# Macaron encoder, fp32 on one core: other sources for the weight sums of the seven-product FFN, one pool for them, and the first block's second pair later

## The chip, the core and the metric

The kernel runs on one core of a Trainium2 chip. The metric is the device time of the whole kernel in microseconds (us). Five engines work side by side, each through its own queue of instructions: TensorE (PE in the profile; PEld are its weight loads), VectorE (DVE), ScalarE (ACT), GpSimd (POOL) and SyncE (SP). The last two do little here but issue DMAs: SP the plain loads of weights, POOL the accumulating DMAs, which add a source to a tile that is in the core's memory (SBUF) already.

## What is computed

A trunk of two layers over 528 tokens (512 and 16 learned ones) of width 1024. Each layer is an FFN, a mixer (gated linear attention beside softmax attention), and an FFN again; the change is in the weights of the four FFNs.

```python
def swiglu(x, w_gate, w_up, w_down):
    return (jax.nn.silu(x @ w_gate) * (x @ w_up)) @ w_down
...
    for l in range(DEPTH):
        h = h + 0.5 * swiglu(rmsnorm(h, norm_gains[l, 0]), ffn_w_gate[l, 0], ffn_w_up[l, 0], ffn_w_down[l, 0])
        h = h + mixer(rmsnorm(h, norm_gains[l, 1]), w_in[l], gla_w2[l], gla_b2[l], gla_gn[l],
                      q_norm[l], k_norm[l], w_pa[l], w_pb[l], b_merge[l], w_out[l], cos, sin)
        h = h + 0.5 * swiglu(rmsnorm(h, norm_gains[l, 2]), ffn_w_gate[l, 1], ffn_w_up[l, 1], ffn_w_down[l, 1])
```

The hidden width is 2816. Everything is float32, and outputs are float32.

## The kernel before

**Products.** A float32 product is made of three matmuls on rounded operands: each operand is split into a high part (rounded to fp32r) and a low part (the rest), and high·high, high·low and low·high are added up. For a weight tile of 128 x 1024 the high part (`whi`) is a cast on ScalarE (L342) and the low part (`wlo`) a subtraction on VectorE (L343).

**Seven products for eight.** The hidden chunks of 128 are taken in 11 pairs (`NPAIR`). For a pair, the gate and up weights are cut into 2 x 2 blocks 11, 12, 21, 22 (512 KB each), the activations into 2 x 2 as well (two halves of the rows, two halves of the tokens), and the block product is made with seven products (Winograd's form of Strassen's scheme) in the order "1627543" or close to it. Three of the seven take a block as it is: "1" takes 11, "2" takes 12, "4" takes 22 (`DIRECT`). Four take sums of blocks:

- "7": s3 = 21 − 11
- "6": s2 = s3 + 22, three blocks
- "5": s1 = 21 + 22, two blocks
- "3": s4 = s2 − 12

The down product of two pairs together (a group, `unit`) is cut the same way and has the same seven products; these are the "S" steps, with block numbers 11 to 14 (`NPAIR + g`), four groups in each FFN, 16 in all. Each step is 24 matmuls on TensorE. In a group, `ffn_steps` writes the order out by hand: the last pair's "7", the group's "1", the pair's "4" and "3", the rest of the group between, and the next pair's "1" and "2". Each S step multiplies a "form" of the two pairs' hidden chunks, which ScalarE and VectorE make after the pair's last product: a cast on ScalarE (L825) and the rest on VectorE (L826), then differences (L831 to L836).

**Where the sums come from** (`sums`, L291). When "1" of a pair or group comes up, ScalarE writes −11 into a tile of pool `wsa` (L284, `negative`); POOL accumulates 21 from DRAM onto it: s3. SP loads 22 into a tile of pool `wsb`, and POOL accumulates s3 onto it: s2. When "2" comes up (for a group: when "1" has been rounded), SP loads 21 into a tile of `wsb` and POOL accumulates 22 from DRAM: s1; and ScalarE writes −12 into `wsa` and POOL accumulates s2 onto it: s4. So a pair takes five loads (11, 12, 22 for "4", and 22 and 21 again), two negatives and four accumulates, and s2 comes after two accumulates in a chain. All accumulates are issued at L289, all loads at L279.

**Order and buffers.** `use` (L353) is called with each step: it makes the high and low parts of the weights a few steps ahead (`make`, up to four and one apart) and fetches two loads further (`fetch`). For the first pair after a group and for every group (`ahead`) the sums are begun as soon as "1" is fetched. The raw blocks have three slots (`raw`) and one apart (`xraw`) that every fourth raw block of the FFNs uses; negatives and loads for sums have three slots each. In the mixer, weights come as plain tiles (`wts`) through the same three raw slots. A load is issued once the slot's last reader, the `wlo` of an earlier block or a negative, is done.

**The first FFN's first block.** Pairs 0 and 1 come first as "F" steps. After the last of them, `hidden` (L781) makes the hidden chunks of both pairs one after the other: scaling by the norm's factor (VectorE, L785), silu (ScalarE, L508), product (VectorE, L802). Chunks of pair 0 go on as plain tiles (L513, L514), those of pair 1 as forms (L825 on).

Of the kernel before, what the change touches and what calls it, by code (L numbers as in the profile page):

```python
# [10 lines left out]
F32 = mybir.dt.float32  # L11
# [53 lines left out]
SQUARES = {(0, "2"): (0, 1, 2, 3), (1, "1"): (4, 5, 6, 7)}  # L65
EARLIEST = ((0, 0), 2, "1")

# [160 lines left out]
class Weights:  # L228
# [3 lines left out]
    def __init__(self, nc, after, raw, hi, lo, wts, win, wdn):  # L232
        self.nc, self.raw, self.hi_pool, self.lo_pool, self.wts, self.win, self.wdn = nc, raw, hi, lo, wts, win, wdn
        self.long = self.short = None
        self.loads = []
        for t, col in zip(PLAN, COLUMN):
            if t[0] == "op":
                self.loads.append(t[1:])
            elif col % SLAB == 0:
                self.loads.append(col // SLAB)  # L240
        self.at = {load: i for i, load in enumerate(self.loads)}
        self.made, self.fetched, self.got, self.summed, self.raws, self.second = 0, 0, {}, {}, {}, {}
        self.pos, self.behind, self.after = 0, None, after
        ops = [i for i, load in enumerate(self.loads) if not isinstance(load, int)]
        self.apart = set(ops[4::5])
        self.raw_apart = set([i for i in ops if self.loads[i][2] in DIRECT][3::4])
        self.extra = None
        firsts = lambda load: [NPAIR + g for g in range(SEVENS)] + [p + 1 for p in lasts(load[0] == (0, 0))]
        self.ahead = [i for i in ops if self.loads[i][2] == "1" and self.loads[i][1] in firsts(self.loads[i])]
        self.chained = {}  # L250

# [22 lines left out]
    def block(self, f, i, name, pool=None, tag="raw"):  # L274

        w = self.slab(tag, pool or self.raw, not pool and self.fetched in self.raw_apart, f"w{name}_{f[0]}{f[1]}_{i}", F32)
        first = f + (i, name) == (0, 0, 0, "11")
# [4 lines left out]
    def negative(self, f, i, name, w):  # L282
        t = self.long.tile([P, SLAB], F32, tag="wsa", name=f"{name}_{f[0]}{f[1]}_{i}")
        self.nc.scalar.activation(t, w, AF.Copy, scale=-1.0)  # L284
        return t

    def add(self, t, src):

        return self.nc.gpsimd.dma_start(t, src, accum_op=ALU.add).ins  # L289

    def sums(self, f, i, product, w):  # L291


        got, before = self.summed, None
        if product == "1":
            s3 = self.negative(f, i, "s3", w)
            self.add(s3, self.dram(f, i, "21"))
            s2 = self.block(f, i, "22", self.short, "wsb")
            before = self.add(s2, s3)
            got[f, i, "7"], got[f, i, "6"], self.second[f, i] = s3, s2, s2  # L300
            self.chained[f, i] = before
        if product == ("ready" if i >= NPAIR else "2"):
            before = self.chained.pop((f, i))
            s1 = self.block(f, i, "21", self.short, "wsb")
            with self.after(before if i >= NPAIR else None):
                self.add(s1, self.dram(f, i, "22"))
            got[f, i, "5"] = s1
        if product == "2":
            s4 = self.negative(f, i, "s4", w)
            self.add(s4, self.second.pop((f, i)))  # L310
            got[f, i, "3"] = s4

    def fetch(self, upto):

        while self.fetched < min(upto, len(self.loads)):
            load = self.loads[self.fetched]
            if isinstance(load, int):
# [3 lines left out]
            elif load[2] in DIRECT:  # L321
                w = self.raws[self.fetched] = self.block(*load[:2], DIRECT[load[2]])
                if load == EARLIEST:
                    self.sums(*load, w)
            self.fetched += 1

    def make(self, upto):
        nc = self.nc
        while self.made < min(upto, len(self.loads)):
# [16 lines left out]
            self.made += 1  # L346
            if not isinstance(load, int) and load != EARLIEST:
                if load[2] == "2" or load[2] == "1" and load[:2] not in self.chained:
                    self.sums(*load, w)
                elif load[2] == "1" and load[1] >= NPAIR:  # L350
                    self.sums(*load[:2], "ready", w)

    def use(self, j):  # L353
        while self.ahead and self.ahead[0] < self.fetched:
            i = self.ahead.pop(0)
            self.sums(*self.loads[i], self.raws[i])
        n = self.room(j)
# [30 lines left out]
def build(tc, ctx, xt, wts, win, wdn, par, w2, const, umask, out):  # L388
# [280 lines left out]
    def ffn(l, f, norm, done, following):  # L669
# [221 lines left out]
        for i, step in enumerate(steps):  # L891
# [8 lines left out]
            elif step[0] == "F":  # L900
# [3 lines left out]
                if step[1:] == (1, "1"):  # L904
                    for j in range(KC // 2):
                        norm.pair(j)
                elif step[1]:
                    rs = factor.pop()
                    for q in range(4):
                        hidden(made[q // 2], q // 2, q % 2)  # L910
            elif step[0] == "O":
# [374 lines left out]
    def block_pools():  # L1286
        pools = open_pools("left", wsa=3, wsb=3, xraw=1, xwhi=1, xwlo=1)
        W.long, W.short, W.extra = pools["wsa"], pools["wsb"], pools
        return pools
# [264 lines left out]
```

## Time and profile before

| | us |
|---|---|
| time, median of three runs (lowest, highest) | 2190.57 (2187.82, 2195.3) |
| the profiled execution: its time | 2200.36 |
| the profiled execution: its span | 2198.6 |
| TensorE busy | 2159.6 |
| VectorE busy | 1716.9 |
| ScalarE busy | 1326.6 |

The profile is of one execution. Its span runs from the first to the last instruction; its time has 1.8 us more around it. Instructions are grouped by line, engine, operation and tiles, without the tiles' numbers: `w<-win` is a load of a gate or up block, `w<-wdn` of a down block, `s<-w` a negative or an accumulate onto one, `w<-s` the accumulate of s3 onto a load, `raw<-wts` a mixer's weight. A bracket behind a row of a timeline holds the time that its engine was idle before it and what ended that time. The granted clock is the share of TensorE's full speed that it was given.

### The profile page before, as it was taken

What the parts mean: (1) busy time and instruction counts of PE and PEld (TensorE: products, weight loads), DVE (VectorE), ACT (ScalarE), POOL (GpSimd) and SP (SyncE); (2) the same over time, 40 slices, a digit from 0 to 9 for tenths busy, and PEclk for the clock granted to TensorE, in tenths of its full rate; (3) what the DMA queues carried; (4) which work ended last, traced back from release to release, by engine and by line L of the source; (5) the groups of instructions that cost most, each with busy time, mean ns of one, the idle gap of its engine ahead of it and who ended that gap; (6) DMA issues with size and microseconds to landing.
All of it is one profiled execution on the core that took longest, in us unless ns stands there. A gap on an engine that the chain in (4) does not pass through costs nothing.

```text
span 2198.6 us, 40509 instructions
## 1 busy us (share of the span) xinstructions
PE 2159.6 (98%) x16572; PEld 2075.3 (94%) x16572; DVE 1716.9 (78%) x2627; ACT 1326.6 (60%) x1964; POOL 203.5 (9%) x236
## 2 busy tenths in 40 slices
PE   9999999999999999999999999999999999999998
PEld 9999999989999999999999999999888889999997
DVE  7888876677977688888698888775789867888885
ACT  8665545455784575656575656454557937656554
POOL 1111100000000011111011111000000001111110
PEclk9999999999999999999999999999999999999999
DMA  9899953211115489999588999532221237999961
GB/s 275 197 232 223 227 134 122 81 59 58 42 48 162 116 211 222 233 237 222 160 198 214 221 234 227 144 125 77 68 68 48 79 113 199 222 221 241 226 170 64
DMA packets 99098, 353.01 MB, mean 161 GB/s; under 512 B 10976, under 2 KB 13280, under 8 KB 98912
## 3 DMA queue, kind: packets, MB, share of 16 engines
q0 software_dynamic: 33408, 121.65, 30.7%
q1 hardware_dynamic: 63424, 225.54, 30.3%
q10 hardware_dynamic: 2080, 3.23, 0.4%
q8 instruction: 130, 2.13, 0.4%
q14 instruction: 56, 0.46, 0.1%
HBM read 287.47 MB, written 2.10 MB: 132 GB/s over the span
## 4 chain that ended last, share of the span: by engine, by line
PE 70%; DVE 9%; ACT 8%; DMA 7%; issue 5%; POOL 0%; DVEq 0%; ACTq 0%; POOLq 0%
PE ss L745 20%; PE ss L864 15%; PE mm L525 13%; PE ss L525 11%; DMA w<-win 5%; DVE wlo L343 3%; PE sm L525 3%; PE ss L700 2%; ACT s L284 2%; ACT whi L342 2%; DMA w<-s 2%; PE sm L1233 1%; ACT t L508 1%; DVE c L760 1%; DMA s<-win 1%
## 5 line engine op out<-in xcount | busy, mean ns | idle before, releaser
L745 PE MATMUL ss<-xc,whi 128*128 128x264 f32 (+1 forms) x4608 | 841.0, 284 | 1.8 <-ACT whi L342 1.8
L745 PEld LDWEIGHTS ss<-xc,whi 128*128 128x128 f32 x4608 | 714.4, 189 | 2.8 <-ACT whi L342 2.0
L745 PE MATMUL ss<-xc,wlo 128*128 128x264 f32 (+1 forms) x2304 | 653.9, 284 | 0.0
L343 DVE TENSOR_TENSOR wlo<-w,whi 128x1024 fp32r<-128x1024 f32 (+1 forms) x299 | 364.0, 1218 | 110.5 <-ACT whi L342 109.6
L745 PEld LDWEIGHTS ss<-xc,wlo 128*128 128x128 f32 x2304 | 434.4, 189 | 0.1
L342 ACT CAST whi<-w 128x1024 fp32r<-128x1024 f32 (+1 forms) x299 | 312.9, 1046 | 200.2 <-PE ss L745 116.8
L525 PE MATMUL mm<-x,whi 128*128 128x264 f32 (+1 forms) x1712 | 383.3, 314 | 0.0
L864 PE MATMUL ss<-g,whi 128*128 128x264 f32 (+1 forms) x1792 | 339.4, 288 | 17.5 <-ACT g L825 12.4
L864 PEld LDWEIGHTS ss<-g,whi 128*128 128x128 f32 x1792 | 283.2, 192 | 23.5 <-ACT g L825 15.1
L525 PEld LDWEIGHTS mm<-x,whi 128*128 128x128 f32 x1712 | 278.2, 188 | 15.8 <-DVE x L514 0.2
L525 PE MATMUL mm<-x,wlo 128*128 128x264 f32 (+1 forms) x856 | 264.3, 313 | 0.0
L864 PE MATMUL ss<-g,wlo 128*128 128x264 f32 (+1 forms) x896 | 256.9, 287 | 0.0
L342 ACT CAST whi<-raw 128x1024 fp32r<-128x1024 f32 x126 | 132.0, 1047 | 142.9 <-PE mm L525 69.1
L343 DVE TENSOR_TENSOR wlo<-raw,whi 128x1024 fp32r<-128x1024 f32 x126 | 153.9, 1222 | 77.7 <-ACT whi L342 76.9
L342 ACT CAST whi<-s 128x1024 fp32r<-128x1024 f32 x116 | 122.0, 1051 | 138.4 <-PE ss L745 73.2
L864 PEld LDWEIGHTS ss<-g,wlo 128*128 128x128 f32 x896 | 171.8, 192 | 0.0
L343 DVE TENSOR_TENSOR wlo<-s,whi 128x1024 fp32r<-128x1024 f32 x116 | 141.6, 1221 | 35.4 <-ACT whi L342 35.4
L525 PEld LDWEIGHTS mm<-x,wlo 128*128 128x128 f32 x856 | 159.6, 188 | 7.5
L284 ACT ACTIVATE s<-w 128x1024 f32<-128x1024 f32 x116 | 122.8, 1059 | 70.9 <-DVE wlo L343 50.4
L868 DVE TENSOR_TENSOR h<-h,ss 128x528 f32<-128x528 f32 (+1 forms) x224 | 153.5, 695 | 6.4 <-PE ss L864 3.4
L525 PE MATMUL ss<-g,whi 128*128 128x264 f32 (+1 forms) x764 | 142.9, 302 | 1.3 <-ACT g L513 1.3
L525 PEld LDWEIGHTS ss<-g,whi 128*128 128x128 f32 x764 | 111.7, 188 | 6.9 <-ACT g L513 1.5
(300 smaller groups left out, 3337.4 us busy)
## 6 DMA issues: line engine op xcount, KB each, us to landing
w<-win SPq DMA_DIRECT2D x217, 512.0 KB, 5.7
raw<-wts SPq DMA_DIRECT2D x126, 512.0 KB, 3.4
w<-wdn SPq DMA_DIRECT2D x80, 512.0 KB, 5.5
w<-s POOLq DMA_DIRECT2D x58, 512.0 KB, 5.7
s<-w POOLq DMA_DIRECT2D x58, 512.0 KB, 8.0
s<-win POOLq DMA_DIRECT2D x42, 512.0 KB, 6.7
w<-win POOLq DMA_DIRECT2D x42, 512.0 KB, 8.1
s<-wdn POOLq DMA_DIRECT2D x16, 512.0 KB, 5.5
```

The costliest lines, as they stand in the source:

```text
L284: self.nc.scalar.activation(t, w, AF.Copy, scale=-1.0)
L342: nc.scalar.copy(hi[:, cs], w[:, cs])
L343: nc.vector.tensor_tensor(lo[:, cs], w[:, cs], hi[:, cs].bitcast(F32), ALU.subtract)
L508: prev_act[0] = S.activation(*args, **kw).ins
L525: TE.matmul(acc.half[i][:width], lhs, rhs[:, acc.spans[i]], start=first, stop=last)
L700: last = TE.matmul(acc[:, t, :w], a[:, j, k], v[b][:, r], start=k == 0 and r == 0 and i == 0, stop=k == len(x) - 1 and r == 1 and i == 2)
L745: TE.matmul(acc[:, j], a[:, j, k], b[:, at], start=bool(begin and k == 0 and i == 0), stop=k == len(x) - 1 and i == 2, skip_group_check=no ...
L760: V.tensor_tensor(st["c"][:, :, q], st["c"][:, :, q], acc, ALU.add)
L864: TE.matmul(acc[:, j], a[:, 2 * half + j, k], b, start=bool(begin and k == 0 and i == 0), stop=k == 1 and i == 2, skip_group_check=not begin)
L868: V.tensor_tensor(to, to, acc, ALU.add)
L1233: TE.transpose(tp[:, j * w + u * n : j * w + (u + 1) * n], pr[:n, (2 * c2 + j) * P : (2 * c2 + j + 1) * P], ident[:n, :n])
```

## The change

The sums come from other sources. s1 = 21 + 22 is made first: SP loads 21 (`base`) and POOL accumulates 22 (`base_sum`), for every group, for the third pair of the first FFN and for the first pair after a group begun two loads (`LEAD`) before "1" is fetched. When "1" is there, ScalarE writes −11 twice: onto the first, POOL accumulates 21 from DRAM (s3), onto the second s1, which gives s2 = 21 + 22 − 11 (`first_sums`). s4 is made as before (`last_sum`). A pair then takes four loads, three negatives and four accumulates, and s2 comes after one accumulate behind its negative. The pools `wsa`, `wsb` and `xraw` go; one pool `ws` of seven slots holds all sums, and all raw blocks go through the three slots of `raw`. In the first FFN the chunks of pair 1 are put off to the end of the next step and alternate with those of pair 0 in the code.

```diff
@@ -63,7 +63,7 @@
 STORES = (((0, 4), (4, 4)), ((0, 1), (1, 2), (3, 3), (6, 2)))
 RESERVED = [((l, f), 1, "5") for l, f in ((0, 1), (1, 0), (1, 1))]
 SQUARES = {(0, "2"): (0, 1, 2, 3), (1, "1"): (4, 5, 6, 7)}
-EARLIEST = ((0, 0), 2, "1")
+LEAD = 2
 
 
 def unit(begin, g):
@@ -231,7 +231,7 @@
 
     def __init__(self, nc, after, raw, hi, lo, wts, win, wdn):
         self.nc, self.raw, self.hi_pool, self.lo_pool, self.wts, self.win, self.wdn = nc, raw, hi, lo, wts, win, wdn
-        self.long = self.short = None
+        self.sum_pool = None
         self.loads = []
         for t, col in zip(PLAN, COLUMN):
             if t[0] == "op":
@@ -243,11 +243,17 @@
         self.pos, self.behind, self.after = 0, None, after
         ops = [i for i, load in enumerate(self.loads) if not isinstance(load, int)]
         self.apart = set(ops[4::5])
-        self.raw_apart = set([i for i in ops if self.loads[i][2] in DIRECT][3::4])
         self.extra = None
-        firsts = lambda load: [NPAIR + g for g in range(SEVENS)] + [p + 1 for p in lasts(load[0] == (0, 0))]
-        self.ahead = [i for i in ops if self.loads[i][2] == "1" and self.loads[i][1] in firsts(self.loads[i])]
-        self.chained = {}
+        self.bases, self.agenda = [], []
+        for i in ops:
+            f, p, product = self.loads[i]
+            if product == "1":
+                early = p >= NPAIR or f == (0, 0) and p == 2 or p - 1 in lasts(f == (0, 0))
+                at = i - LEAD * early
+                self.bases.append((at, (f, p)))
+                self.agenda += [(at, 0, (f, p))] + [(i, 1, (f, p))] * early
+        self.bases.sort()
+        self.agenda.sort()
 
     def dram(self, f, i, name):
         if i >= NPAIR:
@@ -273,55 +279,49 @@
 
     def block(self, f, i, name, pool=None, tag="raw"):
 
-        w = self.slab(tag, pool or self.raw, not pool and self.fetched in self.raw_apart, f"w{name}_{f[0]}{f[1]}_{i}", F32)
+        w = self.slab(tag, pool or self.raw, False, f"w{name}_{f[0]}{f[1]}_{i}", F32)
         first = f + (i, name) == (0, 0, 0, "11")
         for a in np.split(np.arange(SLAB), 2 if first else 1):
             self.nc.sync.dma_start(w[:, a[0] : a[-1] + 1], self.dram(f, i, name)[:, a[0] : a[-1] + 1])
         return w
 
     def negative(self, f, i, name, w):
-        t = self.long.tile([P, SLAB], F32, tag="wsa", name=f"{name}_{f[0]}{f[1]}_{i}")
+        t = self.sum_pool.tile([P, SLAB], F32, tag="ws", name=f"{name}_{f[0]}{f[1]}_{i}")
         self.nc.scalar.activation(t, w, AF.Copy, scale=-1.0)
         return t
 
     def add(self, t, src):
 
-        return self.nc.gpsimd.dma_start(t, src, accum_op=ALU.add).ins
-
-    def sums(self, f, i, product, w):
-
-
-        got, before = self.summed, None
-        if product == "1":
-            s3 = self.negative(f, i, "s3", w)
-            self.add(s3, self.dram(f, i, "21"))
-            s2 = self.block(f, i, "22", self.short, "wsb")
-            before = self.add(s2, s3)
-            got[f, i, "7"], got[f, i, "6"], self.second[f, i] = s3, s2, s2
-            self.chained[f, i] = before
-        if product == ("ready" if i >= NPAIR else "2"):
-            before = self.chained.pop((f, i))
-            s1 = self.block(f, i, "21", self.short, "wsb")
-            with self.after(before if i >= NPAIR else None):
-                self.add(s1, self.dram(f, i, "22"))
-            got[f, i, "5"] = s1
-        if product == "2":
-            s4 = self.negative(f, i, "s4", w)
-            self.add(s4, self.second.pop((f, i)))
-            got[f, i, "3"] = s4
+        self.nc.gpsimd.dma_start(t, src, accum_op=ALU.add)
+
+    def base(self, f, i):
+        self.summed[f, i, "5"] = self.block(f, i, "21", self.sum_pool, "ws")
+
+    def base_sum(self, f, i):
+        self.add(self.summed[f, i, "5"], self.dram(f, i, "22"))
+
+    def first_sums(self, f, i, w):
+        s3, s2 = [self.negative(f, i, n, w) for n in ("s3", "s2")]
+        self.add(s3, self.dram(f, i, "21"))
+        self.add(s2, self.summed[f, i, "5"])
+        self.summed[f, i, "7"], self.summed[f, i, "6"], self.second[f, i] = s3, s2, s2
+
+    def last_sum(self, f, i, w):
+        s4 = self.summed[f, i, "3"] = self.negative(f, i, "s4", w)
+        self.add(s4, self.second.pop((f, i)))
 
     def fetch(self, upto):
 
         while self.fetched < min(upto, len(self.loads)):
+            if self.bases and self.bases[0][0] <= self.fetched:
+                self.base(*self.bases.pop(0)[1])
             load = self.loads[self.fetched]
             if isinstance(load, int):
                 w = self.raw.tile([P, SLAB], F32, tag="raw", name=f"raw{load}")
                 self.nc.sync.dma_start(w, self.wts[load])
                 self.raws[self.fetched] = w
             elif load[2] in DIRECT:
-                w = self.raws[self.fetched] = self.block(*load[:2], DIRECT[load[2]])
-                if load == EARLIEST:
-                    self.sums(*load, w)
+                self.raws[self.fetched] = self.block(*load[:2], DIRECT[load[2]])
             self.fetched += 1
 
     def make(self, upto):
@@ -344,16 +344,19 @@
             self.got[s] = (hi, lo)
             self.got.pop(s - 12, None)
             self.made += 1
-            if not isinstance(load, int) and load != EARLIEST:
-                if load[2] == "2" or load[2] == "1" and load[:2] not in self.chained:
-                    self.sums(*load, w)
-                elif load[2] == "1" and load[1] >= NPAIR:
-                    self.sums(*load[:2], "ready", w)
+            if not isinstance(load, int):
+                if load[2] == "1" and load[:2] not in self.second:
+                    self.first_sums(*load[:2], w)
+                elif load[2] == "2":
+                    self.last_sum(*load[:2], w)
 
     def use(self, j):
-        while self.ahead and self.ahead[0] < self.fetched:
-            i = self.ahead.pop(0)
-            self.sums(*self.loads[i], self.raws[i])
+        while self.agenda and self.agenda[0][0] < self.fetched:
+            i, what, pair = self.agenda.pop(0)
+            if what:
+                self.first_sums(*pair, self.raws[i])
+            else:
+                self.base_sum(*pair)
         n = self.room(j)
         upto = j + n - (j < AHEAD_MADE)
         if not isinstance(self.loads[j], int) and self.loads[j][1:] == (0, "7"):
@@ -906,8 +909,9 @@
                         norm.pair(j)
                 elif step[1]:
                     rs = factor.pop()
-                    for q in range(4):
-                        hidden(made[q // 2], q // 2, q % 2)
+                    for m in range(2):
+                        hidden(made[0], 0, m)
+                        put_off(i + 1, lambda m=m: hidden(made[1], 1, m))
             elif step[0] == "O":
                 two_products(*step[1:])
             elif step[0] == "S":
@@ -1284,8 +1288,8 @@
         norm.pools = open_pools("right", **{"x": dict(x=16), "xc": dict(xc=8)}[kind])
 
     def block_pools():
-        pools = open_pools("left", wsa=3, wsb=3, xraw=1, xwhi=1, xwlo=1)
-        W.long, W.short, W.extra = pools["wsa"], pools["wsb"], pools
+        pools = open_pools("left", ws=7, xwhi=1, xwlo=1)
+        W.sum_pool, W.extra = pools["ws"], pools
         return pools
 
     def decay_weights(l):
```

In the changed file some lines have other numbers: L284 becomes L290, L289 becomes L295, L279 becomes L285, L508 becomes L511, L825 becomes L828, L864 becomes L867; L342 and L343 stay.

Three places show how the instructions move. First ScalarE, at the first product of the second group of the first FFN (block 12). `s_00_6` are negatives for pair 6, `g` is the form that the group's "1" needs, `whi_1920` and `whi_1914` are the high part of the group's "6". Before:

```order
L342 CAST whi_1846<-w_00_5_1784 128x1024
L755 COPY c_1710<-ss_1681 128x2x264
L342 CAST whi_1885<-s_00_5_1624 128x1024
L508 ACTIVATE c_1527<-c_1527 128x528
L342 CAST whi_1920<-w_00_12_1777 128x1024
L284 ACTIVATE s_00_6_2054<-w_00_6_2027 128x1024
L825 CAST g_1878<-c_1527 128x528
L342 CAST whi_1957<-w_00_12_1889 128x1024
```

And after the change:

```order
L342 CAST whi_1840<-w_00_5_1781 128x1024
L758 COPY c_1706<-ss_1675 128x2x264
L342 CAST whi_1879<-s_00_5_1618 128x1024
L511 ACTIVATE c_1524<-c_1524 128x528
L290 ACTIVATE s_00_6_2051<-w_00_6_2024 128x1024
L342 CAST whi_1914<-s_00_12_1773 128x1024
L828 CAST g_1872<-c_1524 128x528
L290 ACTIVATE s_00_6_2053<-w_00_6_2024 128x1024
```

The negative for the next pair now stands ahead of the rounding of the group's "6", and the second negative behind the form.

Second GpSimd, at the first group of the second FFN (`01_11`; `01_3` is the next pair). Before:

```order
L289 DMA s_01_11_9901<-wdn 128x1024
L289 DMA w_01_11_9904<-s_01_11_9901 128x1024
L289 DMA w_01_11_9945<-wdn 128x1024
L289 DMA s_01_11_10088<-w_01_11_9904 128x1024
L289 DMA s_01_3_10181<-win 128x1024
```

And after:

```order
L295 DMA w_01_11_9799<-wdn 128x1024
L295 DMA s_01_11_9890<-wdn 128x1024
L295 DMA s_01_11_9892<-w_01_11_9799 128x1024
L295 DMA s_01_11_10074<-s_01_11_9892 128x1024
L295 DMA w_01_3_10077<-win 128x1024
```

The two-block sum (`w_01_11`, from `wdn`) has moved from third to first, s2 (the row with both 01_11 names) no longer reads s3, and the next pair's two-block sum comes ahead of its s3.

Third ScalarE in the first FFN, behind the first two pairs (`c_322` and `c_582`, after the change `c_319` and `c_576`, are the pairs' chunks; `w_00_3` is block 12, for pair 3's "2"). Before:

```order
L508 ACTIVATE c_322<-c_322 128x528 x2
L508 ACTIVATE c_582<-c_582 128x528 x2
L513 CAST t_779<-c_322 128x528
L342 CAST whi_847<-s_00_2_344 128x1024
L513 CAST t_786<-c_322 128x528
L342 CAST whi_885<-w_00_3_813 128x1024
L825 CAST g_796<-c_582 128x528
```

And after:

```order
L511 ACTIVATE c_319<-c_319 128x528 x2
L342 CAST whi_839<-s_00_2_341 128x1024
L516 CAST t_776<-c_319 128x528
L511 ACTIVATE c_576<-c_576 128x528
L342 CAST whi_875<-w_00_3_798 128x1024
L516 CAST t_783<-c_319 128x528
L511 ACTIVATE c_576<-c_576 128x528
```

The chunks of pair 1 now come between the roundings of the weights.

## The prediction

> **What bounds the kernel now.** The page comes first, for the span and for which engine fills it.
>
> ```profile
> span 2198.6 us, 40509 instructions
> ...
> PE 2159.6 (98%) x16572; PEld 2075.3 (94%) x16572; DVE 1716.9 (78%) x2627; ACT 1326.6 (60%) x1964; POOL 203.5 (9%) x236
> ```
>
> TensorE works in 98% of the span, and the change touches none of its products. So it can win only what TensorE loses: 39 us of idle time, and time at a lower clock. The view of TensorE's waits says where the idle time lies (columns: sum in us, times, longest).
>
> ```profile
> PE ss L864 <- ACT g L825: 12.4, 8, 3.5
> PE ss L864 <- DVE g L826: 4.7, 14, 0.4
> ```
>
> L864 is a group's down product. Its first step ("1") multiplies the form of the pair just finished, which ScalarE rounds (L825) and VectorE completes (L826). 12.4 + 4.7 = 17.1 us are lost there over 16 groups. The timeline of TensorE tells the groups apart; the bracket is the idle time ahead of a row.
>
> ```profile
> 62.07 0.39 PE L745 MATMUL ss<-xc,whi 128*128 128x264 f32 x1 [1.83 <-ACT whi L342]
> 154.99 0.39 PE L864 MATMUL ss<-g,whi 128*128 128x264 f32 x1 [0.33 <-DVE g L826]
> 822.50 0.39 PE L864 MATMUL ss<-g,whi 128*128 128x264 f32 x1 [2.49 <-ACT g L825]
> 823.24 0.59 PE L864 MATMUL ss<-g,whi 128*128 128x264 f32 x1 [0.36 <-DVE g L826]
> 1175.31 0.59 PE L864 MATMUL ss<-g,whi 128*128 128x264 f32 x1 [3.47 <-ACT g L825]
> 1176.05 0.59 PE L864 MATMUL ss<-g,whi 128*128 128x264 f32 x1 [0.16 <-DVE g L826]
> 1898.76 1.31 PE L864 MATMUL ss<-g,whi 128*128 128x256 f32 x2 [3.26 <-ACT g L825]
> 2085.06 0.38 PE L864 MATMUL ss<-g,whi 128*128 128x256 f32 x1 [1.51 <-ACT g L825]
> 2085.79 0.39 PE L864 MATMUL ss<-g,whi 128*128 128x256 f32 x1 [0.34 <-DVE g L826]
> ```
>
> Three stalls (822, 1175, 1898), each in the first group of an FFN after the first, make 2.85 + 3.63 + 3.26 = 9.7 us; the one at 2085 makes 1.85. The other 12 groups, of which 154.99 is a typical one, share what is left: 17.1 − 9.7 − 1.85 = 5.5 us, 0.46 each. A long stall also takes clock. In the view by windows the fourth column is the granted clock, the fifth the DMA share.
>
> ```profile
> 60.00:70.00 10.00, 8.17 (x66) 1.00 0.40 96
> 820.00:830.00 10.00, 7.16 (x45) 0.83 0.94 207
> 1170.00:1180.00 10.00, 6.37 (x34) 0.74 0.87 159
> 1180.00:1190.00 10.00, 10.00 (x78) 0.92 0.91 229
> 1890.00:1900.00 10.00, 6.59 (x50) 0.92 0.97 199
> 1900.00:1910.00 10.00, 10.00 (x67) 0.74 0.99 226
> 2080.00:2090.00 10.00, 8.14 (x53) 0.83 0.96 216
> ```
>
> What is missing to 1.00, times 10 us, is the clock lost: 1.7 at 822, 2.6 + 0.8 = 3.4 at 1175, 3.4 at 1898, 1.7 at 2085, nothing after the 1.83 us at 62. So the three first groups cost 9.7 + 8.5 = 18.2 us and the group at 2085 costs 3.55.
>
> Why the first groups stall is in the timelines of ScalarE and of GpSimd.
>
> ```profile
> 803.55 1.06 ACT L284 ACTIVATE s<-w 128x1024 f32<-128x1024 f32 x1
> ...
> 819.92 1.04 ACT L342 CAST whi<-w 128x1024 fp32r<-128x1024 f32 x1 [3.77 <-DMA w<-s]
> 820.87 1.05 ACT L284 ACTIVATE s<-w 128x1024 f32<-128x1024 f32 x1
> 821.83 0.61 ACT L825 CAST g<-c 128x528 fp32r<-128x528 f32 x1
> ```
>
> ```profile
> 805.01 0.87 POOL L289 DMA_DIRECT2D s<-wdn  x1 [6.76 <-ACT s L284]
> 813.38 0.86 POOL L289 DMA_DIRECT2D w<-s  x1 [7.51 <-DMA s<-wdn]
> ```
>
> The negative of the group's block (803.55) is followed by two accumulates in a chain: s3 += 21, issued at 805.01, and, when that has landed, s2 += s3 at 813.38. s2 is there at 819.9, and the rounding of step "6" stands in ScalarE's queue waiting for it, ahead of the form's rounding at 821.83, for which TensorE waits.
>
> **The change part by part.**
>
> *The two-block sum early, s2 from a second negative.* s2 no longer waits for s3: the sum 21 + 22 is made before, and one accumulate lies between the second negative and s2. Of the 803.55 to 819.92 chain the stretch 805.01 to 813.38 (8.4 us) goes, and a second negative (1.05) and the issue of s3's accumulate (0.87) come in: s2 is there at least 6 us earlier, 814 or before, ahead of the time when ScalarE reaches its rounding. That wait disappears in all three groups. What is late next is the negative of the next pair's block "1" (820.87 before, where it waited for nothing): in the new order it stands ahead of step "6"'s rounding and of the form, and it waits for its raw load. Raw blocks now have three slots, not three and one apart, so this load is issued when the rounding error of the pair's "4" has been taken and its slot comes free.
>
> ```profile
> 811.52 1.23 DVE L343 TENSOR_TENSOR wlo<-w,whi 128x1024 fp32r<-128x1024 f32 x1 [0.24 <-ACT whi L342]
> ...
> 821.00 1.23 DVE L343 TENSOR_TENSOR wlo<-w,whi 128x1024 fp32r<-128x1024 f32 x1 [3.03 <-ACT whi L342]
> 822.48 0.71 DVE L826 TENSOR_TENSOR g<-c,g 128x528 fp32r<-128x528 f32 x1 [0.25 <-ACT g L825]
> ```
>
> That is at 811.52 + 1.23 = 812.75. From the landing L the form needs: the negative (start to next start 821.83 − 820.87 = 0.96), the rounding of "6" until VectorE starts on it (821.00 − 819.92 = 1.08), that "6" error, which now also stands ahead of the form on VectorE (1.14 to the next start), and the form's own (0.71), with 0.1 for starts: L + 4.0. TensorE wants the form's error at 822.50 − 2.49 + 0.38 = 820.39 (0.38 is the work between the two stalls at 822 and 823). So the new stall is L − 816.4.
>
> How long that load takes is the open price. The nearest rows are these.
>
> ```profile
> w<-win SPq DMA_DIRECT2D x217, 512.0 KB, 5.7
> raw<-wts SPq DMA_DIRECT2D x126, 512.0 KB, 3.4
> ```
>
> The same load beside accumulates has a median of 5.7 us, and a load of the same size in the mixer, where little else moves, 3.4. In a first group I take 5.05, nearer to 5.7, since the DMA share there is 0.94: L = 817.8, stall 1.4 (bounds: 0 at 3.4, 2.05 at 5.7). On the clock: 1.85 us at 2085 cost 1.7, 1.83 at 62 cost nothing, so a stall near 1.5 costs half of 1.7, 0.85. The three groups then cost 3 × 2.25 = 6.7 in place of 18.2: **−11.5** (from −18.2 to −7).
>
> The Trainium skill, "TensorE: Matmul & The Clock Gate", section "Part 1: The HAM clock gate", says that TensorE falls to half rate after an idle window of some 3.4 us and that the window runs free. By that alone stalls of 1.4 us would cost no clock, and the three groups would give 2.5 us more. The trace speaks against taking it so: 1.85 us at 2085, in two parts, left 0.83.
>
> *The same wait in the other 12 groups.* Here it is already the raw load that holds ScalarE. Rows of the group at 154: ScalarE, GpSimd, the chain that ended last, VectorE.
>
> ```profile
> 152.61 1.06 ACT L284 ACTIVATE s<-w 128x1024 f32<-128x1024 f32 x1 [0.78 <-DMA w<-win]
> ```
>
> ```profile
> 142.67 0.86 POOL L289 DMA_DIRECT2D w<-s  x1 [4.73 <-DMA s<-wdn]
> 143.29 1.16 POOL L289 DMA_DIRECT2D w<-wdn  x1
> ```
>
> ```profile
> 144.83 7.70 DMA w<-win
> ```
>
> ```profile
> 146.02 1.23 DVE L343 TENSOR_TENSOR wlo<-w,whi 128x1024 fp32r<-128x1024 f32 x1 [0.60 <-ACT whi L342]
> ```
>
> The load leaves at 144.83, right behind two accumulates, takes 7.70 us, lands at 152.53, and the form is 0.33 late. After: it leaves only when the slot of "4" is free, 146.02 + 1.23 = 147.25, which is 2.4 later; and step "6"'s rounding and error stand between it and the form. TensorE wants the error at 154.99 − 0.33 = 154.66, the form needs L + 4.0, so the stall is L − 150.66. For 0.46 as now the load must land in 3.9 us. What speaks for much less than 7.70: the two accumulates are gone from that place. By the new order on GpSimd's and SyncE's queues, s2's is issued some 14 us before the load and s4's some 8 (estimates, from when their inputs are there in the trace of before); only the base sum of the next pair, some 4.5 us before, can still be moving, with one load ahead on the same queue (issued near 144.3). Bounds are 3.4 and 7.70; I take 4.2, near the lower since at most one accumulate overlaps: L = 151.45, stall 0.8, and 12 × (0.8 − 0.46) = **+4** (from −5.5 at 3.4 to +22 and clock at 5.7).
>
> The Trainium skill, "DMA: Bandwidth & Descriptors", section "Anatomy of one DMA", gives for a GpSimd transfer about 2.0 us and bytes over 436 GB/s, an estimate of 3.2 us for 512 KB. By it there would be no stall in these 12 groups and the sum would be about 9.5 lower; the 3.4 row agrees, the 7.70 row does not.
>
> *The group at 2085.* It has the same cause as the 12, with a later load. I take a stall of 1.0 in place of 1.85 and half as much clock lost as after a 1.4: 3.55 becomes 1.5, **−2** (from −3.5 to 0).
>
> *The second pair's hidden chunks of the first FFN later.*
>
> ```profile
> 60.98 1.04 ACT L342 CAST whi<-w 128x1024 fp32r<-128x1024 f32 x1
> ```
>
> The stall at 62.07 waits for the rounding at 60.98, which stands behind all four silus of the two first pairs and both roundings of pair 0's chunks. In the new order one silu and one rounding less stand ahead of it, and TensorE has a whole product of 24 matmuls before it. **−1.8** (the stall; no clock was lost there; worth 0 if VectorE's scaling is what is late).
>
> *Costs off the path.* One negative more in each of 58 sums: 58 × 1.06 = 61 us on ScalarE, which is busy for 60% of the span and in a group does it behind the form. One load fewer in each of 58 sums (five loads and four accumulates become four and four), on DMA engines that the windows show at 0.87 to 0.99: it helps the price of every load above and is counted there. Three raw slots at the starts of the later FFNs: block "1" of pair 0 leaves only behind the mixer's last loads. By the new order and the times of before, ScalarE is held there for up to 1.5 us, and TensorE has its products ready for longer than that; I take nothing, with up to +2 in the range. If that cover is gone, the first product of an FFN starts late by as much.
>
> Sum: −11.5 + 4 − 2 − 1.8 = −11.3. The profiled execution took 2200.36, 9.8 above the median of the three runs; nothing says that the stalls are what differs, so the sum is taken from the median: 2190.57 − 11.3, **2179**.
>
> **The rivals.**
>
> *The raw load becomes the wait in all groups (slower).* One mechanism: three slots make the load of the next pair's "1" leave 2.4 us later, in each of 16 groups, and the form behind its negative, "6"'s rounding and "6"'s error. At 5.7 us, the median of this load now, the stall is 2.3 in the 12 groups: +22, and half of them losing 1.7 of clock, +10; the three first groups gain only 7; 62 gives 1.8: 2190.57 + 23 = 2214. At 5.3 us, half the clock: about 2200. It decides from a price of 4.9 us, where 12 × (1.54 − 0.46) = 13 eats 11.5 + 1.8. For it: 7.70 now. Against: the accumulates have gone from there. I take 2205 for it.
>
> *No change.* At 4.6 us the stall is 1.2, +9 in the 12 groups, and with the first groups at 2.05 and their clock the sum is −7 − 1.8 + 9, about 0 with nothing at 2085: 2190.
>
> *Full relief.* At 3.4 us nothing waits for raw loads: −18.2 − 5.5 − 3.5 − 1.8 = −29, 2162. For it, the mixer's median; against, the DMA share in these windows. This is also what the DMA page's figure would give.
>
> **How the numbers follow.** A measurement of this kernel can tell 0.3% from no change, 6.6 us. The forecast has 0.46, full relief 0.13: faster 0.59. No change has 0.21, slower 0.20. The range reaches from near full relief, 2163, to the slower rival's 2205; the forecast's own is 2170 to 2184.
>
> **What would show it.** Right: in TensorE's waits no first-group stall over 2.1 us, no wait of ScalarE's rounding for a DMA of s2 in those groups, ScalarE's negative waiting for the raw load in most groups, no idle at 62. The load of the next pair's "1" takes 3.4 to 4.9 us, and the granted clock stays at 0.9 or more in the windows of the first groups. Wrong: stalls of 2 us or more in most of the 16 groups, or a new wait at the start of a later FFN, or s2 still the last to come.

## The result and the profile after

The changed kernel takes 2211.67 us (median of 4 runs, 2209.99 to 2215.21), the kernel before, on the same chip, 2192.94 (4 runs, 2187.82 to 2196.87). The ratio is 1.0089 (95% interval 1.0062 to 1.0116): 19 us slower, where 11 us faster was forecast. The profiled execution took 2211.28, with a span of 2209.5.

The page of the kernel after, and the view of TensorE's waits (sum in us, times, longest). Lines of the code stand three lower: L867 was L864.

```profile
span 2209.5 us, 40509 instructions
...
PE 2158.2 (98%) x16572; PEld 2072.5 (94%) x16572; DVE 1719.5 (78%) x2627; ACT 1378.2 (62%) x2022; POOL 204.1 (9%) x236
```

```profile
PE ss L867 <- DVE g L829: 13.1, 16, 0.8
PE ss L867 <- ACT g L828: 12.5, 10, 3.2
PE ss L748 <- ACT c L758: 4.7, 5, 3.0
```

The edit did what it says: by the page's rows of the DMA queues the plain loads moved 195 MB where they had moved 226, and ScalarE works 52 us more. But the wait of a group's "1" for its form has grown from 17.1 to 25.6 us, and VectorE's half of it comes in all 16 groups. The timeline of TensorE shows three of these groups and a new stall in the first FFN.

```profile
65.98 0.81 PE L748 MATMUL ss<-xc,whi 128*128 128x264 f32 x2 [2.96 <-ACT c L758]
...
159.79 0.39 PE L867 MATMUL ss<-g,whi 128*128 128x264 f32 x1 [0.83 <-DVE g L829]
828.43 0.51 PE L867 MATMUL ss<-g,whi 128*128 128x264 f32 x2 [1.33 <-ACT g L828]
829.77 0.39 PE L867 MATMUL ss<-g,whi 128*128 128x264 f32 x1 [0.83 <-DVE g L829]
...
1907.76 0.50 PE L867 MATMUL ss<-g,whi 128*128 128x256 f32 x2 [3.21 <-ACT g L828]
1909.11 0.58 PE L867 MATMUL ss<-g,whi 128*128 128x256 f32 x1 [0.84 <-DVE g L829]
```

What ScalarE waits for ahead of the form is the raw load of the next pair's "1": the chain of waits goes through it in all 16 groups. The first fence is its timeline at the second group, the second is the chain of waits there.

```profile
155.85 1.07 ACT L290 ACTIVATE s<-w 128x1024 f32<-128x1024 f32 x1 [1.00 <-DMA w<-win]
156.82 1.04 ACT L342 CAST whi<-s 128x1024 fp32r<-128x1024 f32 x1
157.76 0.63 ACT L828 CAST g<-c 128x528 fp32r<-128x528 f32 x1
```

```profile
151.46 4.31 DMA w<-win
...
157.89 1.23 DVE wlo L343
159.12 0.63 DVE g L829
```

The load leaves at 151.46, 0.02 us behind the end of the `wlo` of the pair's "4" in the same chain, and lands 4.31 us later; then come the negative, the rounding of "6", its error and the form's own error, as the order of the instructions had it.

Both profiled executions together show only 10.9 us of the 19: the first profile of before (2200.36) was slower than each of its timed runs above. A second one (below) took 2195.42, which leaves 15.9 us.

### The profile page after: what moved, and what is told of

Same layout as the page of the kernel before. It is cut to its first block, busy times and chain, and to the rows that moved or that the text cites. A ratio compares the mean times of both kernels' runs of the same rounds, so it can differ in the third digit from the quotient of the medians.

```text
span 2209.5 us, 40509 instructions
## 1 busy us (share of the span) xinstructions
PE 2158.2 (98%) x16572; PEld 2072.5 (94%) x16572; DVE 1719.5 (78%) x2627; ACT 1378.2 (62%) x2022; POOL 204.1 (9%) x236
## 4 chain that ended last, share of the span: by engine, by line
PE 77%; DVE 9%; ACT 7%; DMA 5%; issue 2%; DVEq 0%; ACTq 0%; SPq 0%
PE ss L748 29%; PE ss L867 14%; PE mm L528 12%; PE ss L528 10%; DMA w<-win 5%; DVE wlo L343 3%; ACT whi L342 3%; PE ss L703 2%; PE sm L528 2%; PE sm L1237 1%; PE ss L1211 1%; ACT t L511 1%; ACT s L290 1%; PE sm L1255 1%; PE sm L1256 1%
## 5 line engine op out<-in xcount | busy, mean ns | idle before, releaser
L342 ACT CAST whi<-w 128x1024 fp32r<-128x1024 f32 (+1 forms) x241 | 252.6, 1048 | 179.3 <-PE ss L748 151.9
L867 PE MATMUL ss<-g,whi 128*128 128x264 f32 (+1 forms) x1792 | 336.5, 287 | 25.6 <-DVE g L829 13.1
L343 DVE TENSOR_TENSOR wlo<-w,whi 128x1024 fp32r<-128x1024 f32 (+1 forms) x241 | 293.5, 1218 | 84.5 <-ACT whi L342 84.1
L867 PEld LDWEIGHTS ss<-g,whi 128*128 128x128 f32 x1792 | 280.6, 190 | 31.6 <-DVE g L829 16.4
L528 PEld LDWEIGHTS mm<-x,whi 128*128 128x128 f32 x1712 | 278.3, 188 | 15.7 <-DVE x L517 0.2
L343 DVE TENSOR_TENSOR wlo<-s,whi 128x1024 fp32r<-128x1024 f32 x174 | 212.6, 1222 | 99.9 <-ACT whi L342 99.6
L342 ACT CAST whi<-s 128x1024 fp32r<-128x1024 f32 x174 | 182.8, 1051 | 131.6 <-PE ss L748 64.5
L867 PE MATMUL ss<-g,wlo 128*128 128x264 f32 (+1 forms) x896 | 255.1, 285 | 0.0
L290 ACT ACTIVATE s<-w 128x1024 f32<-128x1024 f32 x174 | 183.6, 1057 | 73.2 <-DMA w<-win 41.7
L342 ACT CAST whi<-raw 128x1024 fp32r<-128x1024 f32 x126 | 132.3, 1050 | 144.9 <-PE mm L528 69.1
L343 DVE TENSOR_TENSOR wlo<-raw,whi 128x1024 fp32r<-128x1024 f32 x126 | 154.0, 1222 | 78.8 <-ACT whi L342 78.0
L867 PEld LDWEIGHTS ss<-g,wlo 128*128 128x128 f32 x896 | 170.6, 190 | 0.0
```

Source lines behind the costliest of these rows:

```text
L342: nc.scalar.copy(hi[:, cs], w[:, cs])
L343: nc.vector.tensor_tensor(lo[:, cs], w[:, cs], hi[:, cs].bitcast(F32), ALU.subtract)
L528: TE.matmul(acc.half[i][:width], lhs, rhs[:, acc.spans[i]], start=first, stop=last)
L867: TE.matmul(acc[:, j], a[:, 2 * half + j, k], b, start=bool(begin and k == 0 and i == 0), stop=k == 1 and i == 2, skip_group_check=not begin)
```

## The experiments

**The kernel before once more.** No edit.

> The kernel before, unchanged, for a second profile of it. The prediction took the stalls of one execution (2200.36 us), which is 8 to 10 us above the median of the timed runs. If the stalls of the first groups vary between executions, this profile shows TensorE's wait for the group's form (12.4 + 4.7 = 17.1 us and 8.5 us of clock in the first profile) some 5 to 10 us smaller and a time near 2191. If they do not, it shows 17 us again and the time of the execution differs elsewhere. Ratio to before: 1.000.

Measured: 2196.24 us against 2195.19, ratio 1.0009 (0.9996 to 1.0022). Its waits of TensorE, span 2193.6:

```profile
PE ss L864 <- ACT g L825: 11.5, 8, 3.6
PE ss L864 <- DVE g L826: 4.7, 15, 0.4
```

16.2 us of waits for the form in place of 17.1: the stalls of the first groups belong to the kernel and not to one execution. The five us by which the two executions differ are mostly clock (3.4 us less is lost, by the granted clock in windows of 2 us) and 0.9 us of this wait.

**The fourth raw slot back, in the changed kernel.**

```diff
+        self.raw_apart = set([i for i in ops if self.loads[i][2] in DIRECT][3::4])
...
-        w = self.slab(tag, pool or self.raw, False, f"w{name}_{f[0]}{f[1]}_{i}", F32)
+        w = self.slab(tag, pool or self.raw, not pool and self.fetched in self.raw_apart, f"w{name}_{f[0]}{f[1]}_{i}", F32)
...
-        pools = open_pools("left", ws=7, xwhi=1, xwlo=1)
+        pools = open_pools("left", ws=6, xraw=1, xwhi=1, xwlo=1)
```

> The changed kernel with the fourth raw slot back (three and one apart, six sum slots in place of seven). Theory 1, the raw load of the next pair's block 1 leaves later because only three raw slots are left, and ScalarE's negative, the rounding of step 6 and the form stand behind it: the load leaves about 2.4 us earlier in the groups, the wait for the form falls from 25.6 us to below 12, the time by 12 to 20 us, ratio to before 0.998 to 1.003. Rival, the new order on ScalarE alone (the rounding of step 6 and its error ahead of the form): the 0.83 us stalls stay in most groups, the wait stays above 20, the time falls by less than 5 us, ratio 1.006 or more.

Measured: 2175.2 us against 2195.19, ratio 0.9919 (0.9903 to 0.9934), 20 us below the kernel before where the changed kernel is 19 above it: some 39 us, more than the 12 to 20 that theory 1 had asked for. Its page's row of busy times (span 2171.6 us), its largest wait of TensorE, and ScalarE at the second group:

```profile
PE 2145.7 (99%) x16572; PEld 2065.9 (95%) x16572; DVE 1714.9 (79%) x2627; ACT 1376.2 (63%) x2022; POOL 203.2 (9%) x236
```

```profile
PE ss L749 <- ACT c L759: 4.4, 3, 3.0
```

```profile
150.49 1.05 ACT L343 CAST whi<-s 128x1024 fp32r<-128x1024 f32 x1
151.45 1.06 ACT L291 ACTIVATE s<-w 128x1024 f32<-128x1024 f32 x1
152.41 0.62 ACT L829 CAST g<-c 128x528 fp32r<-128x528 f32 x1
```

No group waits for its form any more, the first groups included: the negative finds its block there, without idle time ahead of it. And no clock is lost but at the very end. The largest wait left (3.0 us, at 1865) is of another kind: a negative waits 4.15 us for an accumulate, and the copy stands behind it.

**Only the raw slot taken away, in the kernel before.**

```diff
-        w = self.slab(tag, pool or self.raw, not pool and self.fetched in self.raw_apart, f"w{name}_{f[0]}{f[1]}_{i}", F32)
+        w = self.slab(tag, pool or self.raw, False, f"w{name}_{f[0]}{f[1]}_{i}", F32)
...
-        pools = open_pools("left", wsa=3, wsb=3, xraw=1, xwhi=1, xwlo=1)
+        pools = open_pools("left", wsa=3, wsb=3, xwhi=1, xwlo=1)
```

> The kernel before with only the raw slot apart taken away: three raw slots, six sum slots, the sums made as before. Theory 1, the missing raw slot is what makes the change slow: the load of the next pair's block 1 leaves some 2.4 us later here too and the wait for the group's form grows from 17 us to 30 us or more; time 15 to 45 us over the kernel before, ratio 1.007 to 1.02. Rival, the new order and the extra negatives of the change do it: ratio 0.998 to 1.002, wait for the form near 17 us.

Measured: 2270.61 us against 2198.1, ratio 1.0329 (1.0294 to 1.0364), 72 us slower, more than the 15 to 45 that theory 1 had forecast. The largest wait of TensorE, and the load in the chain at the third group:

```profile
PE ss L864 <- ACT g L825: 55.7, 16, 5.3
```

```profile
218.53 9.54 DMA w<-win
```

The load again leaves right behind the `wlo` of "4", and with the old sums it takes 9.54 us in this group (7.55 to 10.52 in the 13 groups whose chain goes through it). So the raw slot is worth some 39 us with the new sums (18.7 above the kernel before and 20.0 below it) and 72 with the old ones; the rest of the change is worth 20 us with the slot and some 54 (72.5 less 18.7) without it.

**Six sum slots in the changed kernel, as a control.** `ws=7` becomes `ws=6`.

> The changed kernel with six sum slots in place of seven and still three raw slots, as a control for the kernel with the raw slot back, which had six too. Theory 1: as the changed kernel or a little slower, ratio to before 1.008 to 1.014. If the gain of that kernel came from six sum slots (another order of loads), it is near 0.992 here.

Measured: 2216.68 us against 2198.1, ratio 1.0075 (1.0047 to 1.0102), not told apart from 1.0089. The gain with the raw slot does not come from six sum slots. The seventh slot bought nothing that can be measured; with six the waits lie elsewhere, 16.1 + 5.1 = 21.2 us for the form and 8.1 for copies in place of 25.6 and 4.7.

```profile
PE ss L867 <- ACT g L828: 16.1, 14, 2.6
PE ss L748 <- ACT c L758: 8.1, 5, 4.1
PE ss L867 <- DVE g L829: 5.1, 15, 0.4
```

**The memory of one sum more for raw loads.** In the kernel with the raw slot back `ws=6, xraw=1` becomes `ws=5, xraw=2`.

> The changed kernel with two raw slots apart and five sum slots: the memory of one more sum given to raw loads. If raw slots are what matters and six sum slots were more than needed, the time is that of the kernel with one slot apart, ratio 0.990 to 0.993. If sums now wait for slots (there ScalarE's negatives already waited up to 4 us for one at the start of an FFN), stalls of that kind grow and the ratio is 0.995 or more.

Measured: 2288.53 us against 2197.37, ratio 1.041 (1.0373 to 1.0446). Raw slots do not help without limit: now the sums lack room.

```profile
PE ss L749 <- ACT c L759: 37.1, 14, 6.6
PE ss L868 <- ACT g L829: 21.5, 8, 3.9
```

```profile
844.43 1.06 ACT L291 ACTIVATE s<-w 128x1024 f32<-128x1024 f32 x1 [5.17 <-DMA s<-s]
```

The negative waits 5.17 us for the accumulate that frees its slot, and copies and forms stand behind it. That points to the five sum slots; five of them without the second raw slot apart were not tried.

**The form ahead of the negatives and of "6" on ScalarE, in the changed kernel.**

```diff
             def first():
-                parts(u[:, 0:4:2])
+                W.form = parts(u[:, 0:4:2])
...
-        s3, s2 = [self.negative(f, i, n, w) for n in ("s3", "s2")]
+        with self.after(self.form):
+            s3, s2 = [self.negative(f, i, n, w) for n in ("s3", "s2")]
...
+                with self.after(self.form if summed_first else None), self.after(self.behind if load == ((0, 0), 2, "6") or load in RESERVED or summed_first else None):
```

(`parts` returns the form's rounding; `after` holds an instruction behind another in the queue.)

> The changed kernel with the first rounding of the group's form ahead of the two negatives and of the rounding of step 6 on ScalarE; loads and slots as in the changed kernel. Theory 1 and its rival on the order both say that the form then waits for no load: the wait of step 1 for its form falls from 25.6 us to below 5, clock lost in groups from 5 us to nothing, the time by 20 to 28 us, ratio 0.996 to 1.000. If the late load only moves the wait (to the copy of product 7 behind the negative, or to step 6), the time falls by less than 8 us.

Measured: 2207.56 us against 2195.19, ratio 1.006 (1.0045 to 1.0075): 12 us above the kernel before where the changed kernel is 19, so the last case of the expectation. The waits of TensorE, ScalarE at the third group, and its load in the chain:

```profile
PE ss L749 <- ACT c L759: 14.9, 15, 2.6
PE ss L749 <- ACT g L829: 8.3, 9, 1.7
PE ss L749 <- DVE h L873: 4.0, 3, 1.6
```

```profile
221.47 1.06 ACT L290 ACTIVATE s<-w 128x1024 f32<-128x1024 f32 x1 [2.66 <-DMA w<-win]
222.44 0.58 ACT L759 COPY c<-ss 128x528 f32<-128x528 f32 x1
```

```profile
213.21 8.19 DMA w<-win
```

A group's "1" no longer waits for its form, but little is won: now the copy of product "7" stands behind the negative, and 27.2 us of waits stand where 25.6 (form) and 4.7 (copies) were. The order on ScalarE chooses who waits; the late load is what there is to wait for. It isn't a clean test of the order, since the load grew too: 8.19 us where the third group of the changed kernel has 4.92, with the two accumulates issued 2.5 and 1.9 us before it in place of 6.2 and 4.9.

**The first block's second pair as before, in the changed kernel.**

```diff
-                    for m in range(2):
-                        hidden(made[0], 0, m)
-                        put_off(i + 1, lambda m=m: hidden(made[1], 1, m))
+                    for q in range(4):
+                        hidden(made[q // 2], q // 2, q % 2)
```

> The changed kernel with the first block's second pair made as before the change. If putting it off causes the 2.96 us stall at 66 us (and 1.7 us of clock behind it), that stall is gone and the one of 1.8 us at 62 is back: the time falls by 2 to 4 us, ratio to before about 1.007. If the stall comes from the weight sums, it stays and the time is that of the changed kernel, 1.009.

Measured: 2216.47 us against 2195.19, ratio 1.0101 (1.0083 to 1.012), not told apart from 1.0089. A stall of 3.2 us is still there, a little earlier and ended by another instruction:

```profile
63.23 0.51 PE L748 MATMUL ss<-xc,whi 128*128 128x264 f32 x2 [3.20 <-ACT whi L342]
```

**The same edit in the kernel with the raw slot back.**

> The changed kernel with the raw slot back (ratio 0.992) and the first block's second pair made as before the change. Prediction's step: putting it off removes a stall of 1.8 us at 62, so without it the kernel is 1 to 3 us slower, ratio 0.993. Rival: the stall only moved to 63 to 69 (0.5, 0.9 and 0.4 us there), the time is the same, 0.992.

Measured: 2179.34 us against 2198.1, ratio 0.9925 (0.9903 to 0.9947), against 2174.79 for the next kernel on the same chip. By its timeline 3.24 + 0.67 us are idle here between 63 and 66, against 0.47 + 0.91 + 0.41 with the second pair put off:

```profile
63.77 0.51 PE L749 MATMUL ss<-xc,whi 128*128 128x264 f32 x2 [3.24 <-ACT whi L343]
64.95 0.81 PE L749 MATMUL ss<-xc,whi 128*128 128x264 f32 x2 [0.67 <-ACT c L759]
```

So with the new sums the stall behind the first two pairs grows without the put-off, and putting the second pair off holds it at 1.8 us. Without the put-off the kernel is still 19 us faster than the kernel before, so most of the 20 us are due to the sums and their pool.

**The two-block sum not early, in the kernel with the raw slot back.** `LEAD = 2` becomes `LEAD = 0`.

> The changed kernel with the raw slot back and the two-block sum begun with block 1, not two loads earlier. If the early start is what makes s2 ready in the first groups, stalls of 1 us or more come back there and the time rises by 5 to 15 us, ratio 0.994 to 0.999. If one accumulate fewer in the chain is enough by itself, the time stays, 0.992.

Measured: 2174.79 us against 2198.1, ratio 0.9906 (0.9883 to 0.9928). The same time: one accumulate fewer behind the negative is enough, the two loads of lead buy nothing.

**Only the second pair put off, in the kernel before.**

> The kernel before with only the first block's second pair put off, the weight sums and slots as they were. The prediction's step: the 1.8 us stall at 62 goes, time 1 to 2 us lower, ratio 0.999 to 1.000, with no idle of 0.5 us or more between 60 and 70 us. Rival, the part only moves the stall (as where the raw slot is back, 0.5 + 0.9 + 0.4 us between 63 and 69): sum of idle there near 1.8 us, ratio 1.000.

Measured: 2190.0 us against 2197.37, ratio 0.9963 (0.9945 to 0.998). Its stall moved, and shrank by 0.4 us:

```profile
63.98 0.51 PE L745 MATMUL ss<-xc,whi 128*128 128x264 f32 x2 [1.43 <-ACT c L755]
```

Neither side of the expectation is met: the time fell by more (7 us) than that stall has. The profiled execution, 2195.9, was the slowest of the five, and its waits for the form (15.7 us) are near those of before (16.2). Where the rest lies stays open.

## Why the prediction was wrong

The mechanism of the slower rival is what happened: it was priced at 2205 with a chance of 0.20, and its place (the load of the next pair's "1", behind a slot of "4") and its chain (negative, "6", its error, the form) were those of the trace. Its turning point of 4.9 us is also the mean load of the 12 groups, but by its own sum that price gives no change; the longer loads of the first groups and the stall at 62 did the rest. What failed is above all the size of one term, the time of that load, in two places; a second term, at 62, had the wrong sign. Step by step, by the first profile of each kernel:

- **s2 earlier in the first groups: right.** No rounding of "6" waits for s2 any more in the changed kernel, and with the raw slot back nothing of the 18.2 us is left.
- **The stall is L + 4.0 less the wanted time: right.** At the second group the load landed at 155.77, so the form's error should be there at 159.77; TensorE went on at 159.79.
- **The load leaves 2.4 us later, behind two accumulates 8 and 4.5 us earlier and one load: right**, as far as the order goes. At the second group GpSimd issued the accumulate of s4 6.8 us and that of the base sum 4.9 us before it, SyncE its last load 2.9 us before.
- **It takes 4.2 us in the 12 groups and 5.05 in the first ones: wrong.** The chain of waits gives its time in each group; these are the rows of the first group of all and of two of the three first groups behind it (that of the second is above).

```profile
87.06 6.17 DMA w<-win
...
819.86 5.91 DMA w<-win
...
1897.93 7.19 DMA w<-win
```

  Over the 12 groups it is 4.02 to 6.17, mean 4.89; in the three first groups 5.91, 6.36 and 7.19, mean 6.5. The bounds (3.4 and 7.70) held it, but the value was taken near the lower one on the ground that "at most one accumulate overlaps". That ground does not carry it: an accumulate issued 5 us ahead can still be moving, since those of this kind (`w<-win` of POOLq) take a median of 8.6 us here.

```profile
w<-win SPq DMA_DIRECT2D x175, 512.0 KB, 4.6
...
w<-win POOLq DMA_DIRECT2D x42, 512.0 KB, 8.6
```

  For the first groups the value was taken from the two medians and the DMA share, not from the order of issue. What sets them apart in the trace is when the base sum's accumulate was issued; the rows are of the second group of all and of the first group of the second FFN, whose loads left at 151.46 and 819.86:

```profile
146.60 0.87 POOL L295 DMA_DIRECT2D w<-win  x1 [1.06 <-DMA w<-win]
817.55 0.88 POOL L295 DMA_DIRECT2D w<-win  x1 [2.64 <-DVE c L805]
```

  Where it came 4.5 to 5.0 us ahead of the load (12 of the 16 groups) the load took 4.02 to 5.58 us; where it came 2.2 to 3.2 us ahead (the three first groups and the first group of all) it took 5.91 to 7.19. That the accumulate is the cause fits these times; no run took it away. By the load's time the 12 groups lose 14.9 us in place of 5.5: +9.4, not +4, with 1.7 of clock. In the first groups the stalls are 2.2, 2.6 and 4.05, together 8.8 in place of 9.7, and the clock lost falls from 8.5 to 3.4: −6, not −11.5. The Trainium skill, "DMA: Bandwidth & Descriptors", section "Issuing engines are not separate DMA queues", says that transfers started by several engines run on the same DMA engines and interleave. The times of this load by what was issued ahead of it agree.

- **The group at 2085: half right.** The stall is the same (1.86 for 1.85), its clock (1.7) is no longer lost. In the second profile of before it was 1.03 us without loss of clock, so this gain is one between executions.
- **62: wrong in sign.** −1.8 was forecast; the stall became 2.96 us with 1.7 of clock, +2.8. The step counted what stands ahead of one rounding and left out the new negatives in the same queue. ScalarE ahead of the norm's factor (`rs`), in the kernel before and in the changed kernel without the put-off:

```profile
49.81 0.70 ACT L550 ACTIVATE rs<-ss,eps 128x528 f32<-128x528 f32 x1 [1.12 <-PE ss L537]
```

```profile
49.23 1.06 ACT L290 ACTIVATE s<-w 128x1024 f32<-128x1024 f32 x1 [1.60 <-DVE t L535]
50.20 1.03 ACT L342 CAST whi<-w 128x1024 fp32r<-128x1024 f32 x1
51.13 0.69 ACT L553 ACTIVATE rs<-ss,eps 128x528 f32<-128x528 f32 x1
```

  TensorE has the norm's sums ready at 49.5 (49.8 before), but a negative and a rounding now stand ahead of the factor. It starts 1.3 us later, VectorE's scaling also (54.70 in place of 53.39), and the stall is 3.20 in place of 1.83. The prediction had set the step to 0 if the scaling was what is late. In the changed kernel a negative (64.38) also stands right ahead of the copy that ends the stall. With the raw slot back the put-off brings it to 1.8.
- **Starts of the later FFNs: too low.** Nothing was taken; 1.7 us of waits for copies (L758) came in at 786, 792, 1865 and 1870, within the +2 of the range.
- **Cost of ScalarE's negatives: right in the groups, wrong at 62.** With the raw slot back, ScalarE works 50 us more than before and no group waits for its form; behind the first two pairs the negatives cost what is said above.
- **The clock after stalls of some 1.5 us as a coin's toss: held roughly.** In the window rows of the changed kernel, the 2.16 us at 828 lost 1.7 us, the 2.6 us at 1182 nothing, the 1.97 us at 1971 again 1.7; 2.42 us at 95 and 2.11 at 2035 lost nothing either:

```profile
830.00:840.00 10.00, 10.00 (x71) 0.83 0.73 160
1180.00:1190.00 10.00, 7.40 (x59) 1.00 0.66 122
1970.00:1980.00 10.00, 8.03 (x53) 0.83 0.67 129
```

The sum by what was measured: +9.4 + 1.7 − 6 − 1.7 + 2.8 + 1.7 = +8, against 10.9 between the two profiles and −11.3 forecast. Of the 19 us by which this sum lies above the forecast one, the load's time makes two thirds (12 groups 7, first groups 5.5) and the stall at 62 makes 4.6. A part of what is missing between +8 and the measured 19 us of the medians is the choice of the starting point: the sum was hung on the median, while the first profile's stalls and clock were those of an execution 5 us slower than the second one, by which the clock lost in the first groups before is 6.8 and not 8.5. By the second profile the same terms give some +12 (first groups −4, the group at 2085 +0.8), against 15.9 between the profiles. Where the last 3 to 4 us lie stays open.

There was a sign in the working itself that was passed over. Of the three things that the change does, one gave up a resource: the raw slot. What it does was worked out right (2.4 us later, in each of 16 groups), and then it was netted against a hope for shorter loads. Measured alone it is the larger term: it costs some 39 us here and 72 us with the old sums.

## What to carry to other kernels

Where an edit pays for a new use of memory with a buffer of another pool, price the lost buffer by itself, on the longest traced time of its transfer, before netting it against the gain: here the lost raw slot cost 39 us and hid a gain of 20. When an in-order queue waits for a late transfer, moving one victim ahead of the wait (the form) mostly passes the wait to the next (the copy; 6 us were won); here the earlier transfer took it away. The version with the raw slot kept and six sum slots, 2175 us (ratio 0.9919, interval 0.9903 to 0.9934), beats both kernels.

## What the runs showed that was not expected

- One slot of 512 KB decides over 2 to 5 per cent: the fourth raw slot is worth 1.0089 against 0.9919 with the new sums and 1.0329 against 1 with the old ones; five sum slots (with a second raw slot apart) give 1.041, while six or seven (1.0075 and 1.0089) are not told apart.
- A 512 KB load takes 3.4 us in the mixer (median). The load of the next pair's "1" takes 4.02 to 7.19 us in the groups of the changed kernel, 7.47 to 8.95 in those of the kernel before (13 of 16), and 7.55 to 10.52 with the old sums and three raw slots.
- A stall of 2.6 us (1182) lost no clock, one of 1.97 (1971) lost 1.7 us: the length of a stall alone does not say what it costs after.
